# Two attentions of a fused block: units of four heads up to 256 keys, transposes two steps behind the scores, projection quarters in every short step

## The chip, the cores and the metric

The kernel runs on one core of one Trainium2 chip. The metric is device time in microseconds (us), the median of three runs of the kernel before: 1913.82 us (1909.85 to 1915.39). The profile shown is one further execution. Engines are named as the profile names them: PE is TensorE (PEld its weight loads), DVE is VectorE, ACT is ScalarE, POOL is GpSimd, SP is SyncE, which here only issues DMAs.

## The reference, cut to what matters

512 tokens of width 1024 pass four layers in turn. The change touches the attention of the last two. In both, twelve mixing heads of 64 columns (causal with a forget gate in the third layer, dilated in the fourth) and four memory heads over 256 memory tokens end in the same projection:

```python
sc = jnp.einsum('bhqd,bhkd->bhqk', qi, k) * scale       # per block of 128 queries
sc = sc + ci[..., :, None] - c[..., None, :]            # third layer: cumulated log forget gates
sc = jnp.where(kpos[None, :] <= qpos[:, None], sc, NEG)
p = jax.nn.softmax(sc, axis=-1)
out = jnp.einsum('bhqk,bhkd->bhqd', p, v)
...
heads = jnp.concatenate([mix, mem_out], axis=1)
h = h + merge_heads(heads) @ w_out[layer]
h = h + conv_ffn(rmsnorm(h, norm_ffn[layer]), ...)
```

The fourth layer's three dilated branches come to one causal softmax with a table of added logarithms, so both layers share one code path.

## The kernel before

`attn34` (from line 1246) is called twice, for the third and the fourth layer. It projects queries, keys, values and memory, then walks the attention proper (lines 1373 to 1478).

Work is cut into units (line 1454): a block of 128 queries, in the order 3, 2, 0, 1 (line 1453), and a pair of heads `j` (eight pairs; 6 and 7 are the memory heads). A unit of block `qb` has 128, 256, 384 or 512 keys, a memory pair always 256: 32 units in all. The loop of line 1456 makes one step a unit, 34 steps:

- `score` of unit i (line 1382): two matmuls, one for each head on half of the rows of the array, two more that add the forget gates in the third layer; the result lies in a tile `spp` of two PSUM banks, of which there are two. DVE adds the mask and takes the minimum of the negated scores (line 1404; memory heads line 1408), ACT takes the exponential and its sum (line 1409), DVE the reciprocal (line 1412) and the scaled probability (line 1414), in a tile `p2` a head, four of them.
- `value` of unit i - 2 (line 1428): matmuls of values and transposed probabilities into a bank `o` that four pairs share. After the fourth, `group` (line 1441) splits the bank into a high part on ACT (line 1445) and a low part on DVE (line 1446), for a projection in three matmuls.
- `turn_p` of unit i - 1 (line 1416): PE transposes the probabilities into one of two banks `tps`, and `evac` copies them to a tile `pt`, two times in three on ACT (line 361), else on DVE (line 359).
- `steps.tick()` (line 1476): work put off by so many ticks. After the second group of a block `finish` (line 868) is put off by three (line 1449); it makes the output projection in quarters of 24 matmuls of 256 columns, one a tick, into the one bank `misc`, adds two halves to the residual (line 891), then normalises the block (squares on ACT, line 241; sums, a power on POOL, products, lines 242 to 247). Four ticks later the normalised block is transposed in two halves of four, each half through `misc`, and split by ACT and DVE (lines 266 to 270). The last block uses the bank `o` for its second half and leaves its transposes to the next layer's start.

PE's order is written by hand: `Chain` (line 330) makes each score, value, transpose and projection matmul follow the one before it. The transposes of the normalised block and everything on DVE, ACT and POOL are not in the chain; a scheduler places them by program order and readiness. A tile waits until its buffer is free. The projection's weights are loaded and split (lines 204 and 206) while the first units run.

Of the kernel before, what the change touches and what calls it, by code (L numbers as in the profile page):

```python
# [97 lines left out]
def _build(tc, nc, ctx, t, out, dbg, upto):  # L98
    V, A, G, PE = nc.vector, nc.scalar, nc.gpsimd, nc.tensor
# [10 lines left out]
    nrm = pool(ctx, "nrm", 1)  # L110
# [14 lines left out]
    def pst(tag):  # L125
        return banks[tag].tile([128, 512], F32, tag=tag, name=tag)
# [274 lines left out]
    pp = phase(pst_, "prep", side="right")  # L401
# [45 lines left out]
    for half in range(2):  # L447
# [9 lines left out]
        for q in range(2):  # L457
# [8 lines left out]
            tp = pst("ft")  # L466
# [26 lines left out]
    pt = pp.tile([128, 3, 16], F32, name="pt")  # L493
# [287 lines left out]
    steps = Steps()  # L781
# [128 lines left out]
    steps = Steps()  # L910
    chain = Chain()
# [74 lines left out]
    units = [(qb, kv) for qb in range(NB - 1, -1, -1) for kv in range(2)]  # L986
    sts = {qb: {} for qb in range(NB)}
# [258 lines left out]
    def attn34(li, x3, w_in, w_out_ap, gain_next):  # L1246
# [132 lines left out]
        steps = Steps()  # L1379
        chain = Chain()  # L1380

        def score(qb, j, st_):
            qs = slice(qb * 128, qb * 128 + 128)
            nm, sm = st_["nm"], st_["sm"]
            m = 128 * (qb + 1) if j < 6 else 256
            rows = [slice(i * 64, i * 64 + 64) for i in range(2)]
            forget = li == 0 and j < 6
            pp = spp()
            for i, rw in enumerate(rows):
                if j < 6:  # L1390
                    chain.matmul(pp[:, i, :m], qT[rw, j, qs], kT[rw, j, :m], start=True, stop=not forget)
                else:
                    chain.matmul(pp[:, i, :m], qmT[rw, j - 6, qs], kmT[rw, j - 6], start=True, stop=True)
            if forget:
                for i in range(2):
                    chain.matmul(pp[:, i, :m], sel[rows[i], 2 * j + i:2 * j + i + 1].to_broadcast([64, 128]),
                                 c24[rows[i], :m], start=False, stop=True)
            h2 = slice(2 * j, 2 * j + 2)
            for i in range(2):
                hd = 2 * j + i  # L1400
                p2 = ae.tile([128, 512], F32, tag="p2", name="p2", bufs=4)
                src = pp[:, i]
                if j < 6:
                    V.tensor_tensor_reduce(out=p2[:, :m], in0=src[:, :m], in1=nlm[:, 512 - m:], scale=1.0,
                                           scalar=3e38, op0=OP.add, op1=OP.min, accum_out=nm[:, hd:hd + 1])
                    src = p2
                else:
                    V.tensor_reduce(nm[:, hd:hd + 1], src[:, :m], axis=AX.X, op=OP.min)
                A.activation(p2[:, :m], src[:, :m], AF.Exp, bias=nm[:, hd:hd + 1], scale=-1.0,  # L1409
                             accum_out=sm[:, hd:hd + 1])  # L1410
                st_[hd] = p2
            V.reciprocal(sm[:, h2], sm[:, h2])
            for hd in (2 * j, 2 * j + 1):
                V.tensor_scalar(st_[hd][:, :m], st_[hd][:, :m], sm[:, hd:hd + 1], None, op0=OP.mult)

        def turn_p(qb, j, st_):
            m = 128 * (qb + 1) if j < 6 else 256
            st_["pt", j] = []
            for i in range(2):
                p2 = st_[2 * j + i]  # L1420
                tp = tps()
                for kb in range(m // 128):
                    chain.transpose(tp[:, kb * 128:(kb + 1) * 128], p2[:, kb * 128:(kb + 1) * 128], ident)
                pt_ = ae.tile([128, 512], F32, tag="pt", name="pt_", bufs=2)
                evac(pt_[:, :m], tp[:, :m])
                st_["pt", j].append(pt_)

        def value(qb, j, st_):
            m = 128 * (qb + 1) if j < 6 else 256
            jj = j % 4  # L1430
            if jj == 0:
                st_["po", j // 4] = pst("o")
            pov = st_["po", j // 4].rearrange("p (j q) -> p j q", j=4)
            for kb in range(m // 128):
                for i in range(2):
                    hd = 2 * j + i
                    vv = vt[:, kb, hd * 64:(hd + 1) * 64] if j < 6 else vm[:, kb, (hd - 12) * 64:(hd - 11) * 64]
                    chain.matmul(pov[i * 64:(i + 1) * 64, jj], vv, st_["pt", j][i][:, kb * 128:(kb + 1) * 128],
                                 start=kb == 0, stop=kb == m // 128 - 1)

        def group(qb, hg, st_):
            po = st_["po", hg]
            ah = ap_.tile([128, 4, 128], F32R, tag="ah", name="ah", bufs=3)
            al = ap_.tile([128, 4, 128], F32R, tag="al", name="al", bufs=3)
            A.activation(f3(ah), po, AF.Copy)
            V.tensor_tensor(f3(al), po, f3(ah).bitcast(F32), op=OP.subtract)
            st_["a", hg] = (ah, al)
            if hg == 1:
                steps.later(3, lambda: finish(
                    steps, wo, lambda k: (st_["a", k // 4][0][:, k % 4], st_["a", k // 4][1][:, k % 4]), qb, gb, xn_,  # L1450
                    qb == order[-1], ap_ if order.index(qb) % 2 else nrm, chain))

        order = (3, 2, 0, 1)
        units = [(qb, j) for qb in order for j in range(8)]
        sts = {qb: {} for qb in range(NB)}
        for i in range(len(units) + 2):
            if i in (1, 2):
                q = int(i == 2)
                ps = pst("misc")
                fm(ps, w, q * 128, 128, xk(x3))  # L1460
                A.activation(qmT[:, q], ps, AF.Copy, scale=-0.125)
            if i < len(units):
                qb, j = units[i]
                if j == 0:
                    sts[qb]["nm"] = ae.tile([128, 16], F32, tag="nm", name="nm", bufs=2)
                    sts[qb]["sm"] = ae.tile([128, 16], F32, tag="sm", name="sm", bufs=2)
                score(qb, j, sts[qb])
# [174 lines left out]
```

## Time and profile before

| what | us |
|---|---|
| median of three runs (1909.85 to 1915.39) | 1913.82 |
| the profiled execution | 1911.97 |
| its span, first to last instruction | 1910.2 |
| attention of the third layer, first score matmul to first projection matmul of the last block | 732.65 to 867.40 |
| attention of the fourth layer, the same | 1381.30 to 1519.04 |

Times within the span are counted from its start. In rows of a stretch, the first number is its length, then the busy time of each engine with its number of instructions; a busy PE need not be PE at its peak, since matmuls are pipelined and their ends modelled. PEclk is the share of full clock that the throttle granted.

### The profile page before, as it was taken

How to read it: one execution, taken by the hardware profiler on the slowest of the kernel's cores; microseconds unless marked ns; L12 is line 12 of the kernel's file. 1: busy time of each engine (PE TensorE's matmuls, PEld its weight loads, DVE VectorE, ACT ScalarE, POOL GpSimd, SP SyncE). 2: the span in 40 equal slices, each digit the busy share in tenths (PEclk: the TensorE clock that was granted, in tenths of full speed). 3: DMA queues.
4: the chain of work that ended last, by engine and by line, in shares of the span. 5: the costliest groups of instructions: out<-in, count | busy, mean ns of one | idle time of the engine just before them, and what ended most of it. 6: DMA issues, size and time to landing. Idle time of an engine off the chain costs nothing.

```text
span 1910.2 us, 27945 instructions
## 1 busy us (share of the span) xinstructions
PE 1806.0 (95%) x11106; PEld 1512.9 (79%) x11108; DVE 1043.8 (55%) x2201; ACT 731.5 (38%) x1456; POOL 139.3 (7%) x151
## 2 busy tenths in 40 slices
PE   6799799999999999999999999999989999999998
PEld 5787578768789886778888888899957788888886
DVE  5985564279555534655655563265375565554522
ACT  4233353333443334543443342133264444333421
POOL 1452001213120000000000000000000000000000
PEclk9899989969999999999999999999998999999999
DMA  5303412301512442003333323342220043332321
GB/s 176 100 24 100 142 36 62 100 22 57 179 54 75 125 122 77 13 1 91 102 107 89 89 81 106 100 144 93 69 84 1 3 130 103 89 94 83 110 88 67
DMA packets 187899, 161.75 MB, mean 85 GB/s; under 512 B 14568, under 2 KB 170320, under 8 KB 187768
## 3 DMA queue, kind: packets, MB, share of 16 engines
q1 hardware_dynamic: 181168, 144.30, 24.6%
q0 software_dynamic: 2784, 9.00, 1.6%
q10 hardware_dynamic: 3816, 6.66, 1.1%
q8 instruction: 88, 1.44, 0.3%
q14 instruction: 43, 0.35, 0.1%
HBM read 157.88 MB, written 4.74 MB: 85 GB/s over the span
## 4 chain that ended last, share of the span: by engine, by line
PE 76%; DVE 10%; issue 5%; ACT 4%; DMA 3%; POOL 2%; ACTq 0%; POOLq 0%; DVEq 0%; SPq 0%
PE acc L212 19%; PE acc L210 19%; PE acc L211 19%; PE misc L339 6%; PE o L339 3%; PE tps L339 2%; PE spp L339 2%; DVE wl L206 2%; PE sps L1096 1%; ACT wh L204 1%; PE misc L210 1%; POOL rstd L234 1%; PE misc L211 1%; PE misc L212 1%; ACT p L1409 1%
## 5 line engine op out<-in xcount | busy, mean ns | idle before, releaser
L206 DVE TENSOR_TENSOR wl<-raw,wh 128x1024 fp32r<-128x1024 f32 (+3 forms) x250 | 300.6, 1211 | 402.6 <-ACT wh L204 401.9
L204 ACT ACTIVATE wh<-raw 128x1024 fp32r<-128x1024 f32 (+2 forms) x262 | 270.8, 1044 | 483.3 <-PE acc L211 211.6
L212 PE MATMUL acc<-xh,wl 128*128 128x512 f32 (+2 forms) x1064 | 400.4, 377 | 4.9 <-DVE wl L206 4.9
L210 PE MATMUL acc<-xh,wh 128*128 128x512 f32 (+2 forms) x1064 | 401.1, 379 | 1.2 <-ACT wh L204 0.7
L211 PE MATMUL acc<-xl,wh 128*128 128x512 f32 (+2 forms) x1064 | 400.5, 377 | 1.2 <-DVE xl L270 1.0
L212 PEld LDWEIGHTS acc<-xh,wl 128*128 128x128 f32 (+1 forms) x1064 | 200.5, 188 | 45.6 <-DVE wl L206 6.5
L210 PEld LDWEIGHTS acc<-xh,wh 128*128 128x128 f32 (+1 forms) x1064 | 199.8, 189 | 41.0 <-ACT wh L204 1.1
L211 PEld LDWEIGHTS acc<-xl,wh 128*128 128x128 f32 (+1 forms) x1064 | 200.5, 189 | 39.7 <-DVE xl L270 1.2
L210 PE MATMUL acc<-wh,xh 128*128 128x256 f32 (+1 forms) x704 | 206.5, 294 | 12.3 <-DVE u L359 10.2
L212 PE MATMUL acc<-wh,xl 128*128 128x256 f32 (+1 forms) x704 | 202.9, 288 | 0.6 <-DVE xl L270 0.6
L211 PE MATMUL acc<-wl,xh 128*128 128x256 f32 (+1 forms) x704 | 201.7, 287 | 0.9 <-DVE wl L206 0.9
L210 PEld LDWEIGHTS acc<-wh,xh 128*128 128x128 f32 x704 | 136.2, 193 | 17.5 <-DVE u L359 10.4
L212 PEld LDWEIGHTS acc<-wh,xl 128*128 128x128 f32 x704 | 136.2, 193 | 5.7 <-issue 4.4
L212 PE MATMUL acc<-wh,gl 128*128 128x512 f32 x352 | 139.2, 395 | 0.0
L210 PE MATMUL acc<-wh,gh 128*128 128x512 f32 x352 | 138.5, 394 | 0.0
L211 PE MATMUL acc<-wl,gh 128*128 128x512 f32 x352 | 138.5, 393 | 0.0
L211 PEld LDWEIGHTS acc<-wl,xh 128*128 128x128 f32 x704 | 136.3, 194 | 1.8 <-DVE wl L206 1.1
L245 POOL TENSOR_TENSOR rs<-ss,mhalf 128x1 f32<-128x1 f32 x32 | 17.6, 551 | 1463.8 <-DVE ss L243 1447.7
L339 PE MATMUL misc<-wh,ah 128*128 128x256 f32 x280 | 82.4, 294 | 0.0
L339 PE MATMUL misc<-wl,ah 128*128 128x256 f32 x280 | 79.4, 283 | 0.0
L339 PE MATMUL misc<-wh,al 128*128 128x256 f32 x280 | 79.1, 282 | 0.0
L211 PEld LDWEIGHTS acc<-wl,gh 128*128 128x128 f32 x352 | 66.2, 188 | 15.6
(1501 smaller groups left out, 3065.9 us busy)
## 6 DMA issues: line engine op xcount, KB each, us to landing
raw<-in_w_up_dram SPq DMA_DIRECT2D x176, 256.0 KB, 3.2
raw<-in_w_down_dram SPq DMA_DIRECT2D x44, 512.0 KB, 3.6
raw<-in_od_w_in_dram SPq DMA_DIRECT2D x24, 512.0 KB, 3.6
raw<-in_w_in_dil_dram SPq DMA_DIRECT2D x20, 512.0 KB, 3.9
raw<-in_ev_w_in_dram SPq DMA_DIRECT2D x18, 512.0 KB, 4.3
raw<-in_w_out_dram SPq DMA_DIRECT2D x16, 512.0 KB, 3.8
raw<-in_w_in_fox_dram SPq DMA_DIRECT2D x14, 512.0 KB, 4.3
raw<-in_ev_w_out_dram SPq DMA_DIRECT2D x8, 512.0 KB, 4.2
```

Of the source, the lines that this page charges most:

```text
L204: A.activation(hi[:, k0:k1], raw, AF.Copy)
L206: eng.tensor_tensor(lo[:, k0:k1], raw, hi[:, k0:k1].bitcast(F32), op=OP.subtract)
L210: pe.matmul(ps, lh, rh, start=first, stop=False)
L211: pe.matmul(ps, lh, rl, start=False, stop=False)
L212: pe.matmul(ps, ll, rh, start=False, stop=last)
L234: G.tensor_tensor(r2[:, :n], r[:, :n], mhalf[:, :n], op=OP.pow)
L245: G.tensor_tensor(r, ss[:, 3:4], mhalf[:, :1], op=OP.pow)
L339: self.last = op(*a, **k).ins
L1096: PE.matmul(ps[:, :n], qiT[rw, hd // 2, qs], kiT[rw, :n], start=True, stop=True)
L1409: A.activation(p2[:, :m], src[:, :m], AF.Exp, bias=nm[:, hd:hd + 1], scale=-1.0, accum_out=sm[:, hd:hd + 1])
```

## The change

A unit becomes a block and a tuple of head pairs: one pair as before for the mixing heads of blocks 2 and 3, two pairs (four heads) for the memory heads of every block and for all heads of blocks 0 and 1. Two pairs lie side by side in the columns of the same `spp`, `p2`, `tps` and `pt` tiles. A step now makes the score of unit i, the value of unit i - 3 and the transposes of unit i - 2; `p2` has six buffers. `finish` is put off by one tick, which is the tick of the same step, and the normalised block always lies in the tile of the pool `nrm`, which has one buffer, where it alternated with a second tile. The quarters of the projection come one a tick, as before.

```diff
+        def width(qb, js):
+            return 128 * (qb + 1) if js[0] < 6 else 256
+
+        def score(qb, js, st_):
...
+            m = width(qb, js)
...
+            forget = li == 0 and js[0] < 6
+            cols = [slice(a * m, a * m + m) for a in range(len(js))]
             pp = spp()
...
+            for j, cl_ in zip(js, cols):
+                for i, rw in enumerate(rows):
+                    if j < 6:
+                        chain.matmul(pp[:, i, cl_], qT[rw, j, qs], kT[rw, j, :m], start=True, stop=not forget)
+                    else:
+                        chain.matmul(pp[:, i, cl_], qmT[rw, j - 6, qs], kmT[rw, j - 6], start=True, stop=True)
+                if forget:
+                    for i in range(2):
+                        chain.matmul(pp[:, i, cl_], sel[rows[i], 2 * j + i:2 * j + i + 1].to_broadcast([64, 128]),
+                                     c24[rows[i], :m], start=False, stop=True)
+            ps_ = [ae.tile([128, 512], F32, tag="p2", name="p2", bufs=6) for _ in range(2)]
+            for j, cl_ in zip(js, cols):
                 for i in range(2):
...
-                p2 = ae.tile([128, 512], F32, tag="p2", name="p2", bufs=4)
...
+                    hd = 2 * j + i
+                    p2, src = ps_[i][:, cl_], pp[:, i, cl_]
+                    if j < 6:
+                        V.tensor_tensor_reduce(out=p2, in0=src, in1=nlm[:, 512 - m:], scale=1.0,
+                                               scalar=3e38, op0=OP.add, op1=OP.min, accum_out=nm[:, hd:hd + 1])
+                        src = p2
+                    else:
+                        V.tensor_reduce(nm[:, hd:hd + 1], src, axis=AX.X, op=OP.min)
+                    A.activation(p2, src, AF.Exp, bias=nm[:, hd:hd + 1], scale=-1.0, accum_out=sm[:, hd:hd + 1])
+            h2 = slice(2 * js[0], 2 * js[-1] + 2)
             V.reciprocal(sm[:, h2], sm[:, h2])
...
+        def turn_p(qb, js, st_):
+            n = width(qb, js) * len(js)
...
+            for p2 in st_["p", js]:
                 tp = tps()
-                for kb in range(m // 128):
+                for kb in range(n // 128):
...
-                evac(pt_[:, :m], tp[:, :m])
+                evac(pt_[:, :n], tp[:, :n])
...
+        def value(qb, js, st_):
+            nk = width(qb, js) // 128
+            if js[0] % 4 == 0:
+                st_["po", js[0] // 4] = pst("o")
...
+            for a, j in enumerate(js):
+                for kb in range(nk):
+                    for i in range(2):
...
+                        ks = slice((a * nk + kb) * 128, (a * nk + kb + 1) * 128)
+                        chain.matmul(pov[i * 64:(i + 1) * 64, j % 4], vv, st_["pt", js][i][:, ks],
+                                     start=kb == 0, stop=kb == nk - 1)
...
             if hg == 1:
-                steps.later(3, lambda: finish(
+                steps.later(1, lambda: finish(
                     steps, wo, lambda k: (st_["a", k // 4][0][:, k % 4], st_["a", k // 4][1][:, k % 4]), qb, gb, xn_,
-                    qb == order[-1], ap_ if order.index(qb) % 2 else nrm, chain))
+                    qb == order[-1], nrm, chain))
 
         order = (3, 2, 0, 1)
-        units = [(qb, j) for qb in order for j in range(8)]
+        units = [(qb, js) for qb in order
+                 for js in ([(0, 1), (2, 3), (4, 5)] if qb < 2 else [(j,) for j in range(6)]) + [(6, 7)]]
         sts = {qb: {} for qb in range(NB)}
-        for i in range(len(units) + 2):
+        for i in range(len(units) + 3):
...
-            if i > 1:
-                qb, j = units[i - 2]
-                value(qb, j, sts[qb])
-                if j % 4 == 3:
-                    group(qb, j // 4, sts[qb])
-            if 0 < i <= len(units):
-                qb, j = units[i - 1]
-                turn_p(qb, j, sts[qb])
+            if i > 2:
+                qb, js = units[i - 3]
+                value(qb, js, sts[qb])
+                if js[-1] % 4 == 3:
+                    group(qb, js[-1] // 4, sts[qb])
+            if 1 < i <= len(units) + 1:
+                qb, js = units[i - 2]
+                turn_p(qb, js, sts[qb])
             steps.tick()
```

## Rows read from the trace of the kernel before

**Rows 1.** The page, part 1: busy us (share of span) and instructions by engine

```profile
PE 1806.0 (95%) x11106; PEld 1512.9 (79%) x11108; DVE 1043.8 (55%) x2201; ACT 731.5 (38%) x1456; POOL 139.3 (7%) x151
```

**Rows 2.** Stretches of the third layer's attention: length, busy us, clock, DMA

```profile
749.12:770.11 20.99, 17.16 (x120) 10.99 (x119) 16.68 (x39) 13.76 (x29) 0.00 (x0) 0.84 0.50 151
802.83:813.04 10.21, 8.27 (x76) 5.61 (x75) 8.34 (x32) 6.70 (x24) 0.55 (x1) 1.00 0.00 0
813.04:829.85 16.81, 16.59 (x143) 14.70 (x142) 7.80 (x36) 6.35 (x28) 0.00 (x0) 1.00 0.00 1
829.85:840.25 10.40, 8.93 (x75) 6.02 (x74) 9.17 (x32) 7.12 (x24) 0.55 (x1) 1.00 0.01 2
859.72:867.40 7.68, 5.44 (x45) 3.57 (x44) 5.42 (x12) 3.72 (x11) 0.55 (x1) 1.00 0.01 2
```

**Rows 3.** Stretches of the fourth layer's attention, each from a first score matmul

```profile
1394.58:1415.67 21.09, 16.77 (x142) 10.59 (x141) 18.68 (x40) 16.50 (x32) 0.00 (x0) 1.00 0.47 150
1448.41:1460.92 12.51, 10.50 (x69) 6.70 (x68) 8.61 (x32) 6.65 (x24) 0.55 (x1) 0.75 0.00 0
...
1478.97:1491.84 12.87, 10.85 (x70) 6.37 (x69) 9.55 (x34) 7.60 (x25) 0.55 (x1) 0.87 0.00 1
1510.35:1519.03 8.68, 6.55 (x45) 4.45 (x44) 5.75 (x13) 3.45 (x10) 0.55 (x1) 0.83 0.01 2
```

**Rows 4.** PE's timeline from 1448.41: start, duration, line, operation, idle before

```profile
1449.05 0.32 PE L339 MATMUL o<-pt__13462,vt 128*64 128x128 f32 x1
...
1449.85 0.66 PE L339 MATMUL tps<-ident,p 128*128 128x128 f32 x4
1450.44 0.49 PE L339 MATMUL spp<-kT,qT 64*128 64x128 f32 x4
1450.86 0.43 PE L339 MATMUL o<-pt__13526,vm 128*64 128x128 f32 x2
...
1451.79 0.63 PE L266 MATMUL misc<-ident,xn 128*128 128x128 f32 x4
1453.83 0.66 PE L266 MATMUL misc<-ident,xn 128*128 128x128 f32 x4 [1.41 <-DVE xl L270]
```

**Rows 5.** PE's timeline of a tight step, from 1478.97

```profile
1479.60 0.32 PE L339 MATMUL o<-pt__13788,vt 128*64 128x128 f32 x1
...
1479.97 0.66 PE L339 MATMUL tps<-ident,p 128*128 128x128 f32 x4
1480.56 0.70 PE L339 MATMUL spp<-kT,qT 64*128 64x256 f32 x4
```

**Rows 6.** Waits of PE, third layer's attention: total us, times, longest

```profile
PE tps L339 <- DVE p L1414: 2.5, 7, 0.7
PE misc L266 <- DVE xl L270: 1.4, 1, 1.4
PE o L339 <- ACT pt__7377 L361: 1.1, 1, 1.1
```

**Rows 7.** Waits of PE, fourth layer's attention

```profile
PE tps L339 <- DVE p L1414: 4.5, 8, 0.9
PE misc L266 <- DVE xl L270: 2.8, 2, 1.4
```

**Rows 8.** Timeline: last value matmul of a group, and the group's split on DVE

```profile
793.86 0.27 PE L339 MATMUL o<-pt__7705,vt 128*64 128x128 f32 x1
...
796.76 0.68 DVE L1446 TENSOR_TENSOR al<-o,ah 128x512 fp32r<-128x512 f32 x1
...
1422.80 0.27 PE L339 MATMUL o<-pt__13200,vm 128*64 128x128 f32 x1
...
1424.24 0.68 DVE L1446 TENSOR_TENSOR al<-o,ah 128x512 fp32r<-128x512 f32 x1
```

**Rows 9.** Copies of transposes on DVE, 512 and 256 columns: busy us, mean ns

```profile
L359 DVE COPY pt__7495<-tps 128x512 f32<-128x512 f32 x1 | 0.7, 690 | 1.0 <-PE tps L339 1.0
L359 DVE COPY pt__8218<-tps 128x256 f32<-128x256 f32 x1 | 0.4, 425 | 0.3 <-PE tps L339 0.3
```

More of the change, by code (lines that the diff above doesn't have):

```diff
@@ L1380, in attn34 @@
         chain = Chain()
-        def score(qb, j, st_):
+        def width(qb, js):
+            return 128 * (qb + 1) if js[0] < 6 else 256
+        def score(qb, js, st_):
             qs = slice(qb * 128, qb * 128 + 128)
             nm, sm = st_["nm"], st_["sm"]
-            m = 128 * (qb + 1) if j < 6 else 256
+            m = width(qb, js)
             rows = [slice(i * 64, i * 64 + 64) for i in range(2)]
-            forget = li == 0 and j < 6
+            forget = li == 0 and js[0] < 6
+            cols = [slice(a * m, a * m + m) for a in range(len(js))]
@@ L1388, in score @@
             pp = spp()
[L1389 to L1394, printed above, removed]
-                for i in range(2):
-                    chain.matmul(pp[:, i, :m], sel[rows[i], 2 * j + i:2 * j + i + 1].to_broadcast([64, 128]),
-                                 c24[rows[i], :m], start=False, stop=True)
@@ L1398, in score @@
-            h2 = slice(2 * j, 2 * j + 2)
-            for i in range(2):
-                hd = 2 * j + i
-                p2 = ae.tile([128, 512], F32, tag="p2", name="p2", bufs=4)
[L1402 to L1411, printed above, removed]
@@ L1412, in score @@
-            V.reciprocal(sm[:, h2], sm[:, h2])
[L1413 to L1420, printed above, removed]
+            for j, cl_ in zip(js, cols):
[8 more added lines that the diff above has]
+                                     c24[rows[i], :m], start=False, stop=True)
@@ L1421, in turn_p @@
+            h2 = slice(2 * js[0], 2 * js[-1] + 2)
+            V.reciprocal(sm[:, h2], sm[:, h2])
+            for j, cl_ in zip(js, cols):
+                for i in range(2):
+                    hd = 2 * j + i
+                    V.tensor_scalar(ps_[i][:, cl_], ps_[i][:, cl_], sm[:, hd:hd + 1], None, op0=OP.mult)
+            st_["p", js] = ps_
+        def turn_p(qb, js, st_):
+            n = width(qb, js) * len(js)
+            st_["pt", js] = []
+            for p2 in st_["p", js]:
                 tp = tps()
-                for kb in range(m // 128):
+                for kb in range(n // 128):
@@ L1423, in turn_p @@
                     chain.transpose(tp[:, kb * 128:(kb + 1) * 128], p2[:, kb * 128:(kb + 1) * 128], ident)
                 pt_ = ae.tile([128, 512], F32, tag="pt", name="pt_", bufs=2)
-                evac(pt_[:, :m], tp[:, :m])
[L1426 to L1439, printed above, removed]
+                evac(pt_[:, :n], tp[:, :n])
@@ new lines, in turn_p @@
+                st_["pt", js].append(pt_)
+        def value(qb, js, st_):
+            nk = width(qb, js) // 128
+            if js[0] % 4 == 0:
+                st_["po", js[0] // 4] = pst("o")
+            pov = st_["po", js[0] // 4].rearrange("p (j q) -> p j q", j=4)
+            for a, j in enumerate(js):
+                for kb in range(nk):
+                    for i in range(2):
+                        hd = 2 * j + i
+                        vv = vt[:, kb, hd * 64:(hd + 1) * 64] if j < 6 else vm[:, kb, (hd - 12) * 64:(hd - 11) * 64]
+                        ks = slice((a * nk + kb) * 128, (a * nk + kb + 1) * 128)
+                        chain.matmul(pov[i * 64:(i + 1) * 64, j % 4], vv, st_["pt", js][i][:, ks],
+                                     start=kb == 0, stop=kb == nk - 1)
@@ L1462, in attn34 @@
             if i < len(units):
-                qb, j = units[i]
-                if j == 0:
+                qb, js = units[i]
+                if js[0] == 0:
                     sts[qb]["nm"] = ae.tile([128, 16], F32, tag="nm", name="nm", bufs=2)
                     sts[qb]["sm"] = ae.tile([128, 16], F32, tag="sm", name="sm", bufs=2)
-                score(qb, j, sts[qb])
-            if i > 1:
-                qb, j = units[i - 2]
-                value(qb, j, sts[qb])
-                if j % 4 == 3:
-                    group(qb, j // 4, sts[qb])
-            if 0 < i <= len(units):
-                qb, j = units[i - 1]
-                turn_p(qb, j, sts[qb])
+                score(qb, js, sts[qb])
+            if i > 2:
[6 more added lines that the diff above has]
+                turn_p(qb, js, sts[qb])
             steps.tick()
```

## The prediction

> **What bounds the kernel now.** The first part of the page gives the share of each engine: TensorE (PE) is busy for 95% of the span [rows 1]. That says little about the two attentions, because the end of a matmul is modelled and a short one counts for longer than it holds the array. So I cut each attention into stretches at the first score matmul of a step (a pass of the unit loop) and asked for the busy time of each engine in them. The reader is to see three kinds of stretch. Where every step carries a quarter of the output projection, PE idles 0.22 us in 16.81 us for four steps [rows 2]: nothing to win. Where the first query block (512 keys) runs beside the splitting of the projection's weights, VectorE (DVE) is busy 16.68 of 20.99 us in the first attention and 18.68 of 21.09 us in the second [rows 2, 3]: DVE sets most of that pace. Between two projections, and behind the last unit, PE idles in both: 1.94 of 10.21 us, 2.01 of 12.51 us and so on [rows 2, 3]. There the granted TensorE clock also drops: it is 0.75, 0.87 and 0.83 over three such stretches of the second attention, so part of each ran at 1.2 instead of 2.4 GHz after PE had idled [rows 3].
>
> The timeline tells what such a step should take. A tight one, of two heads without projection, starts its scores at 1478.97, where a stretch begins [rows 3], its values at 1479.60, its transposes at 1479.97 and the next scores at 1480.56: 0.63 + 0.37 + 0.59 = 1.59 us [rows 5]. Another, from 1448.41, goes 0.64 + 0.80 + 0.59 us with six value pairs instead of two [rows 3, 4], so a value pair costs (0.80 - 0.37) / 4 = 0.108 us and the group a fixed 0.15. Scores for 128 keys take 0.42 us [rows 4] against 0.63 for 256, so 0.21 per 128 keys and 0.21 fixed. Four transposes at about the price of a value pair are 0.43, so of their 0.59 some 0.16 is fixed (an estimate). **A two-head step thus pays about 0.52 us for changing from scores to values to transposes and back**, whatever its width.
>
> With these prices I rebuild the stretches. The four steps from 1448.41 are 2.03 + 1.59 + 1.37 + 1.16 = 6.15 us, the eight transposes of the normalised block 8 x 0.11 = 0.88; measured 12.51, so 5.5 us are waits [rows 3, 4]. The same sum gives 7.0 + 0.88 of 12.87 (waits 5.0) for the other stretch [rows 3], and in the first attention, whose scores have a third matmul pair (0.06 to 0.12 us more), 6.3 + 0.88 of 10.21 (waits 3.0) and 7.35 + 0.88 of 10.40 (2.2) [rows 2]. Together 15.7 us in sixteen steps. Behind the last unit (scores, three value groups, two transpose groups, the eight transposes: 4.43 us) the stretches last 7.68 and 8.68 us: 3.25 + 4.25 = 7.5 us of waits [rows 2, 3]. **So 23.2 us of waits stand in six short stretches.** Who is late: the transposes wait for the scaled probabilities, 2.5 us in seven places and 4.5 us in eight [rows 6, 7], and the second half of the normalised block waits 1.41 us for the copy of the first out of the one bank "misc" [rows 4, 7]. The rest is values that wait for the copied transposes.
>
> **The change part by part.** No matmul, exponential or byte of DMA is added; PE's order is written by hand (the chain), and nothing passes another instruction on SP's queue, and POOL has only the power of each norm, as before.
>
> *Four-head units.* Units fall from 32 to 7 + 7 + 4 + 4 = 22 for each attention: ten score, value and transpose groups less in each, 20 in both. At 0.52 us that is 10.4 us at most, and 0 at least, if a merged unit pays the fixed part again between its two head pairs, which no row shows. The tight steps all show the fixed part at a change of kind, so I take a value near the upper end: **-8 us**. The copies of the transposes become half as many and twice as wide (0.69 us for 512 columns, 0.42 for 256 [rows 9]); the reciprocals halve. Both lie on DVE and ScalarE (ACT) beside a PE that is the bound in steps with a quarter: 0. If that cover goes, a copy is 0.27 us later.
>
> On that the Trainium skill speaks against the change: "Perfetto Trace Analysis", section "Optimizing Scalar/DVE Operations", says that when those engines are not saturated but cause bubbles elsewhere, breaking instructions up helps, and grouping pays when they are. The trace has DVE busy for 8.34 of 10.21 us there [rows 2], nearer to the second condition. By the first, six merged steps without a quarter would lose 6 x 0.27 = 1.6 us, and the sum below would be -18.4 instead of -20.0.
>
> *Quarters in every short step.* With two fewer ticks before `finish` and four steps for a block, the quarters fill steps 9 to 12 and then 16 to 27 of a loop of 25 and its drain; before they filled 11 to 14, 19 to 22, 27 to 30 and 35 to 38. The sixteen waiting steps become six without a quarter (13 to 15 in each attention), and the last values and transposes go between quarters. What stays of the 23.2 us: the six steps at 0.8 us (15.7 / 16 = 1.0 now, less 0.2 since a whole step more lies before the transposes): 4.8 us. And the eight transposes of query block 2 now fall between the last quarter of block 0 and the first of block 1, all through "misc": the residual add (0.69 by the width of the other 512-column DVE rows), then twice 2.04 us from half to half [rows 4], 4.8 us in all, of which 0.88 is work and 1.0 covered by the values of the last unit (0.15 + 8 x 0.108): 2.9 us, twice 5.8. So 23.2 - 10.6 = **-12.6 us**, with bounds of -18.4 (no squeeze) and -7.5 (the tails alone).
>
> *Transposes two steps behind, six probability tiles.* The waits for scaled probabilities add up to 7.0 us [rows 6, 7], most of them in the stretches counted already. Outside, DVE at 80 to 89% stays what it is [rows 2, 3], and the values still come one step behind the transposes, so the wait passes on to the copies: **-1 us**, bounds 0 and -4. The two more tiles hold the unit that is now in flight; scores still wait for the two score banks, as before.
>
> *The first quarter in the step of its group.* Its first 12 matmuls read the older half of the heads; the other 12 need the split of the group just finished. From the last value matmul to the end of the split 2.12 us pass in one place (1422.80 to 1424.92) and 3.58 in another (793.86 to 797.44) [rows 8]. Transposes (0.59) and half a quarter (a step with quarter is 16.81 / 4 = 4.2 us [rows 2], a step like it without 1.2, so 1.5 for the half) cover 2.1 us. Bounds 0 and 1.5 us for each of eight blocks; the later one had norm work on ACT ahead of it, the earlier not. Of the eight groups those of blocks 0 and 1 come one step behind a norm: 0.4 each for these four, 0 for the others, **+1.6 us**. Queued behind that wait on PE are the next scores, by the chain.
>
> *One normalised tile for all blocks.* Block 0's squares must wait for block 2's transposes; by the count above they end 4.8 us after block 0's last quarter, and the result is needed only behind quarters of 3 us each: 0. If that cover went, the squares, two small sums, the power on POOL and the two products would stand in a row, and the start of the next layer's work would wait.
>
> Sum: -8 - 12.6 - 1 + 1.6 = **-20.0 us** against the profiled execution's 1911.97 us (span 1910.2 and 1.8 around it; 1.85 under the median 1913.82 of the three runs): **1892 us**. A measurement of this kernel can tell about 0.3% (5.7 us) from no change.
>
> **The rivals.**
>
> *The wait moves on (1905.6).* The probabilities are ready sooner, but the copies behind them are not, and every wait of the six stretches reappears one engine later, in the steps with a quarter. Only the removed steps count: -8 + 1.6 = -6.4. For it: in the 512-key stretch late copies stand in front of values, the longest by 1.1 us [rows 6], and DVE is 80 to 89% busy. Against it: steps with a quarter show no such waits today [rows 2]. Chance 0.20. With one squeeze more in each attention it is no change (1912), chance 0.13, which also holds the case that the order on DVE and ACT, which is not written by hand, undoes the longer lag.
>
> *"misc" becomes the bound (1920).* From step 16 on that bank carries quarters without a pause, and all three blocks' transposes must squeeze through it, each pair costing 0.69 + 2 x 2.04 = 4.8 us of which 0.9 is work. If none is covered, that is 6 x 3.9 = 23.4 us, where such pairs cost 1.4 + 2.8 = 4.2 now by waits of this kind [rows 6, 7]. The scores stand behind the blocked quarter in the chain, so of the gain only the removed steps and a part of the tails (-5 of 7.5) are left: -8 + 1.6 - 5 + 23.4 - 4.2 = +7.8. It decides once a pair costs more than 3 us and the lag wins nothing. Against it: those transposes are outside the chain and stand a step or two ahead of their place in the program today [rows 4]. Chance 0.08. The Trainium skill ("Perfetto Trace Analysis", section "Matmuls") asks independent groups to rotate through banks, so that the copy of one overlaps the matmuls of the next; the 1.41 us idle [rows 4] agree with what happens otherwise.
>
> *More than counted (under 1881).* No wait left and the clock at 2.4 GHz throughout: -10.4 - 18.4 - 4 = -33, 1879. Chance 0.04.
>
> **How the numbers follow.** The forecast (1881 to 1900) has 0.55, the moved wait 0.20, no change 0.13, slower 0.08, more 0.04. Faster by over 0.3%: 0.55 + 0.20 + 0.04 = 0.79; within it 0.13; slower 0.08. The range runs from 1881 to 1909, past the first rival.
>
> **What would show it.** Right: the stretches with all units of 128 and 256 keys have PE idle under 1 us in ten, the clock row stays near 1.00 from the second block on, and "tps waits for p L1414" falls from 7.0 to under 2 us. The squeeze: a wait of "misc" quarters for the copies of the normalised block, near the end of each attention. Wrong: the same idle time with the copies of transposes as releasers, or first quarters that wait for the split by over 1 us.

## The result and the profile after

The changed kernel takes 1900.9 us (median of six runs, 1897.92 to 1905.28) against 1910.8 beside it: ratio 0.9942, 95% interval 0.993 to 0.9954. Its profiled execution took 1900.18 us, the one of before 1911.97. First the page's part 1, to be held against [rows 1]: PE is busy for 14.7 us less in all.

```profile
PE 1791.3 (94%) x11108; PEld 1513.8 (80%) x11108; DVE 1036.1 (55%) x2167; ACT 728.5 (38%) x1430; POOL 138.8 (7%) x151
```

The two profiled executions, cut at the start of an attention's first score matmul, of its last projection matmul, and of the first Silu of the feed-forward behind it (us; worked out from the timelines; attention 4 is cut at 1380.76 before, its first score matmul, a half microsecond ahead of the 1381.30 of the table above):

| | to attention 3 | attention 3 | to Silu | to attention 4 | attention 4 | to Silu | rest |
|---|---|---|---|---|---|---|---|
| before | 732.65 | 146.03 | 29.06 | 473.02 | 149.73 | 29.66 | 349.99 |
| after | 735.41 | 149.70 | 25.96 | 473.49 | 137.87 | 25.95 | 349.98 |

Attention 4 gained 11.9 us, **attention 3 lost 3.7**, and 3.1 + 3.7 us came from the start of the feed-forwards, which the forecast had at nothing. (The first column and the fourth are code that the change does not touch. Over all kept traces of this document they take 732.65 to 738.76 and 472.21 to 476.73 us, so differences of a few us there say nothing.) A part of the difference between the two attentions is PE's clock: it stood at its lower level for 6.8 and 17.1 us of them before, for 13.7 and 3.4 us after.

Stretches of the changed kernel, with the columns of [rows 2, 3]. The first covers five steps near the start of attention 3; those from 813.03 and 1448.37 begin at a first score matmul; the last begins behind the transposes of block 2's normalised block:

```profile
747.42:770.62 23.20, 18.15 (x138) 12.16 (x136) 17.52 (x38) 16.42 (x31) 0.00 (x0) 0.93 0.44 136
...
813.03:826.92 13.89, 9.08 (x62) 7.92 (x62) 5.59 (x23) 4.65 (x17) 0.00 (x0) 0.77 0.00 0
...
1448.37:1459.82 11.45, 9.73 (x90) 6.96 (x89) 9.44 (x38) 8.16 (x30) 0.55 (x1) 1.00 0.01 2
1507.28:1512.60 5.32, 4.09 (x34) 3.98 (x34) 3.40 (x7) 3.72 (x7) 0.55 (x1) 1.00 0.04 12
```

At the start DVE is busy for 17.52 of 23.20 us, five steps; in [rows 2] for 16.68 of 20.99, four steps. One step of attention 3, from 813.03, takes 13.89 us at a mean clock of 0.77, where the step behind it, with a quarter as well, takes 5.2. The main waits of PE in attention 3, then in attention 4 (total us, times, longest), against [rows 6, 7]:

```profile
PE misc L266 <- DVE xl L270: 4.4, 2, 3.4
PE o L339 <- DVE pt__7355 L359: 4.3, 1, 4.3
PE misc L339 <- DVE xl L270: 2.6, 2, 1.4
PE o L339 <- DVE al L1454: 1.8, 2, 1.4
...
PE misc L339 <- DVE al L1454: 1.1, 2, 0.9
```

```profile
PE o L339 <- DVE al L1454: 2.6, 2, 1.4
PE o L339 <- ACT pt__12918 L361: 2.6, 1, 2.6
PE misc L266 <- DVE xl L270: 2.3, 2, 1.2
...
PE misc L339 <- DVE xl L270: 1.2, 1, 1.2
PE misc L339 <- DVE al L1454: 0.9, 2, 0.7
```

The wait for scaled probabilities, 7.0 us before, is gone from both attentions. Others have grown. Values wait 11.6 us for copied transposes, 9.4 before (the sums of all such waits in both attentions), and 4.4 us for the split that empties their bank "o" (`al`), 0.8 before. The bank "misc" costs 4.4 + 2.6 + 2.3 + 1.2 = 10.5 us of waits around the transposes of normalised blocks. The long step of attention 3 on PE's timeline (start, duration, line, operation, idle before):

```profile
815.77 0.27 PE L266 MATMUL misc<-ident,xn 128*128 128x128 f32 x1
819.44 0.66 PE L266 MATMUL misc<-ident,xn 128*128 128x128 f32 x4 [3.40 <-DVE xl L270]
821.50 0.58 PE L339 MATMUL misc<-wh,ah 128*128 128x256 f32 x1 [1.41 <-DVE xl L270]
821.88 0.41 PE L339 MATMUL misc<-wl,ah 128*128 128x256 f32 x1
822.10 0.41 PE L339 MATMUL misc<-wh,al 128*128 128x256 f32 x1
```

The last transpose of block 3's first half starts at 815.77; the second half can start only at 819.44 and the first quarter of block 2 at 821.50. Its matmuls then come every 0.21 us where they come every 0.12 elsewhere: the trace has the clock at half from 820.4 to 827.2. The quarter takes 5.42 us, to the next scores, where others take 3.0. What the first half's copy (the last line) stood behind, on DVE:

```profile
816.98 0.87 DVE L1421 TENSOR_SCALAR p<-p,sm 128x128 f32<-128x128 f32 x4
817.77 0.68 DVE L1454 TENSOR_TENSOR al<-o,ah 128x512 fp32r<-128x512 f32 x1
818.37 0.41 DVE L359 COPY pt__7977<-tps 128x256 f32<-128x256 f32 x1
818.70 0.68 DVE L270 TENSOR_TENSOR xl<-misc,xh 128x512 fp32r<-128x512 f32 x1
```

And the start of the feed-forward behind attention 4, DVE's timeline before, then after:

```profile
1530.81 0.69 DVE L891 TENSOR_TENSOR h<-o,h 128x512 f32<-128x512 f32 x1 [4.02 <-PE o L339]
1531.42 1.22 DVE L206 TENSOR_TENSOR wl<-raw,wh 128x1024 fp32r<-128x1024 f32 x1
```

```profile
1511.46 2.35 DVE L206 TENSOR_TENSOR wl<-raw,wh 128x1024 fp32r<-128x1024 f32 x2
1514.72 0.69 DVE L891 TENSOR_TENSOR h<-misc,h 128x512 f32<-128x512 f32 x1 [0.91 <-PE misc L339]
```

Before, the first up-projection slab (a tile of weights) was split (`wl`) behind the last block's last residual add, and PE waited 2.0 us in three places for such splits. After, both pieces of it are split ahead of the first half's add, and PE has no such wait.

### The profile page after: what moved, and what is told of

Its sections match the earlier page's. It is cut to its first block, busy times and chain, and to the rows that moved or that the text cites. A ratio compares the mean times of both kernels' runs of the same rounds, so it can differ in the third digit from the quotient of the medians.

```text
span 1898.4 us, 27786 instructions
## 1 busy us (share of the span) xinstructions
PE 1791.3 (94%) x11108; PEld 1513.8 (80%) x11108; DVE 1036.1 (55%) x2167; ACT 728.5 (38%) x1430; POOL 138.8 (7%) x151
## 4 chain that ended last, share of the span: by engine, by line
PE 78%; DVE 8%; issue 5%; ACT 4%; DMA 3%; POOL 1%; ACTq 0%; POOLq 0%; DVEq 0%; SPq 0%
PE acc L212 20%; PE acc L210 20%; PE acc L211 20%; PE misc L339 6%; PE o L339 3%; PE tps L339 2%; DVE wl L206 1%; PE spp L339 1%; PE sps L1096 1%; DMA raw<-in_w_in_dil_dram 1%; ACT wh L204 1%; ACT p L1415 1%; PE misc L210 1%; PE misc L211 1%; PE misc L212 1%
## 5 line engine op out<-in xcount | busy, mean ns | idle before, releaser
L210 PEld LDWEIGHTS acc<-wh,xh 128*128 128x128 f32 x704 | 135.9, 193 | 18.4 <-DVE u L359 10.4
L210 PE MATMUL acc<-wh,gh 128*128 128x512 f32 x352 | 138.5, 394 | 0.0
L211 PE MATMUL acc<-wl,gh 128*128 128x512 f32 x352 | 138.5, 393 | 0.0
```

The source lines that it names most:

```text
L210: pe.matmul(ps, lh, rh, start=first, stop=False)
L211: pe.matmul(ps, lh, rl, start=False, stop=False)
```

## The experiments

Ratios are to the kernel before, timed on the same chip in the same rounds. Its median beside store_only to x_by_tps is 1915.6, beside lag_one_x to store_x 1915.2, beside empty_tile to lag_one_x_pool 1911.3, beside x_a_step_earlier 1914.8. Stage lengths of every profiled execution:

| run | ratio (95%) | attention 3 | to Silu | attention 4 | to Silu |
|---|---|---|---|---|---|
| the change | 0.9942 (0.993 to 0.9954) | 149.70 | 25.96 | 137.87 | 25.95 |
| store_only | 0.9943 (0.9926 to 0.9961) | 143.98 | 25.77 | 152.99 | 25.77 |
| pairs | 0.997 (0.9958 to 0.9982) | 149.14 | 25.77 | 146.47 | 25.77 |
| lag_one | 0.99 (0.9886 to 0.9915) | 143.10 | 25.42 | 142.01 | 25.73 |
| x_by_tps | 0.9888 (0.9874 to 0.9903) | 140.38 | 26.00 | 138.03 | 26.00 |
| lag_one_x | 0.9881 (0.9861 to 0.9902) | 141.02 | 25.77 | 138.46 | 26.00 |
| lag_one_p4 | 0.997 (0.9954 to 0.9985) | 141.49 | 31.26 | 138.76 | 32.03 |
| x_lo_on_pool | 0.9883 (0.9863 to 0.9904) | 140.25 | 25.76 | 135.20 | 25.77 |
| store_x | 1.004 (1.0025 to 1.0055) | 150.75 | 25.78 | 154.07 | 26.00 |
| empty_tile | 0.9957 (0.9943 to 0.997) | 144.06 | 25.76 | 146.78 | 25.77 |
| lag_only | 0.9972 (0.9958 to 0.9986) | 145.77 | 25.95 | 147.58 | 25.70 |
| lag_one_x_pool | 0.9881 (0.9867 to 0.9894) | 139.67 | 25.76 | 139.58 | 25.77 |
| x_a_step_earlier | 0.9947 (0.9933 to 0.9961) | 146.98 | 26.02 | 142.18 | 25.77 |

The attentions of the kernel before, of store_only and of empty_tile have the same instructions on PE in the same order; they took 144.0 to 146.0 and 146.8 to 153.0 us. So one attention of one execution is good to some 3 us, and the starts of the feed-forward (25.4 to 26.0 wherever they are early) to a few tenths.

**store_only**: the storage alone, on the kernel before.

```diff
-                p2 = ae.tile([128, 512], F32, tag="p2", name="p2", bufs=4)
+                p2 = ae.tile([128, 512], F32, tag="p2", name="p2", bufs=6)
...
-                    qb == order[-1], ap_ if order.index(qb) % 2 else nrm, chain))
+                    qb == order[-1], nrm, chain))
```

> The kernel before with only the storage of the change: six probability tiles and one normalised tile; units, lag and quarters as before, PE's order in the two attentions unchanged. Theory A (the feed-forward starts gained 3.1 and 3.7 us in the changed kernel because the six probability tiles push the projection's weights out of the memory of the first up-projection slab, so that its splits no longer stand behind the last block's residual add): about 1904 to 1905 against 1911 (ratio 0.9965), all of it between the last projection matmul and the first Silu (29.1 and 29.7 become about 26). Rival B (those 6.8 us come from the earlier norm of block 0, that is from the units and quarters): no difference (ratio 1.000), the stretches stay at 29.

Both starts fell to 25.77: theory A. The median fell further than these 7.2 us (1902.6 from 1915.6); the ratio's interval, 7.5 to 14.2 us, begins just above them, and no trace here shows where the rest comes from. **The storage alone is worth about as much as the whole change.**

**empty_tile**: the kernel before with one normalised tile, four probability tiles, and beside them memory that nothing uses.

```diff
         ae = phase(stx, "ae")
+        ae.tile([128, 1024], F32, tag="pad", name="pad", bufs=1)
```

> The kernel before with one normalised tile and an empty tile of 4096 bytes a partition, which nothing reads or writes, beside its four probability tiles: the memory of six tiles without the tiles. Units, lag, quarters and PE's order in the attentions as before. If it is the place of the projection's weights in memory that starts the feed-forward earlier: 25.8 us in both starts instead of 29.1 and 29.7, 1902 to 1905 in all, as with six tiles (0.9943). If two more tiles to write into gave the gain: 1910 to 1914 and starts of 29.

The starts are 25.76 and 25.77. The kernel needs the place, not the tiles (nor is it the one normalised tile: lag_one_p4 below has it too, without the place, and starts late). DVE's timeline of this run has the split of the slab ahead of the adds, as after the change:

```profile
1517.24 2.36 DVE L206 TENSOR_TENSOR wl<-raw,wh 128x1024 fp32r<-128x1024 f32 x2 [1.68 <-ACT wh L204]
1520.05 0.69 DVE L891 TENSOR_TENSOR h<-misc,h 128x512 f32<-128x512 f32 x1 [0.46 <-PE misc L339]
```

The code agrees: the pool `ae` with six probability tiles, two copies and its small sums is 16,640 bytes a partition, exactly the two tiles of the slab in the pool `wx`, which takes that place next; with four it is 4,096 less, and the slab reaches into the pool `wo`, which holds weights of the projection that is still running.

**lag_one**: transposes one step behind the scores, as before the change.

```diff
-        for i in range(len(units) + 3):
+        for i in range(len(units) + 2):
...
-            if i > 2:
-                qb, js = units[i - 3]
+            if i > 1:
+                qb, js = units[i - 2]
...
-            if 1 < i <= len(units) + 1:
-                qb, js = units[i - 2]
+            if 0 < i <= len(units):
+                qb, js = units[i - 1]
```

> The changed kernel with the transposes one step behind the scores as before (a loop one step shorter); four-head units, six tiles, first quarter in the step of its group stay. By the forecast's term the lag is worth 1 us: 1901 to 1903 (changed kernel: 1901). If the lag is what lets the merged units work, the waits of transposes for scaled probabilities come back (7 us before, nearly none now) and it is 1905 to 1908. If the copies are late anyway, the longer lag only costs its extra step at the end and this is 1898 to 1900.

1896.2 us, below all three: the interval of the ratio, 0.9886 to 0.9915, lies under that of the change, so the longer lag made the change slower. In attention 3 its long step takes 6.79 us, not 13.89, since the scheduler placed block 3's transposes a step sooner. (Attention 4 of this profile takes 142.0 us, 4 more than in the change.)

**lag_one_p4**: lag_one with `bufs=4` for `p2`.

> The kernel with transposes one step behind, with four probability tiles instead of six (one step of lag needs no more). It takes away only the storage. Theory A (six tiles keep the first up-projection slab clear of the projection's weights): both feed-forward starts go back from 25.4 and 25.7 to about 29, the attentions stay within 3 us of 143 and 142, in all 6 to 8 us over the 1896 of six tiles: 1902 to 1904. Rival B (the starts come from the units and quarters): 25.5 to 26 stay, 1896.

The starts went to 31.26 and 32.03, the time to 1906.8: theory A, at nearly twice the price. In the start behind attention 4 PE waits 0.9 us for splits on DVE and 3.4 for those on ACT; the longest of these waits, 2.8 us, ends with a split before which ACT had idled 4.88 us for the weights' DMA. Units and early quarters without the storage are worth 0.3%.

**pairs**: two heads a unit again.

```diff
-                 for js in ([(0, 1), (2, 3), (4, 5)] if qb < 2 else [(j,) for j in range(6)]) + [(6, 7)]]
+                 for js in [(j,) for j in range(8)]]
```

> The changed kernel with units of two heads everywhere; lag of two steps, six tiles, one normalised tile and first quarter in the step of its group stay. It takes away the merged units and with them the quarters in every short step. Theory A: what is left is the storage (-6.5) and the lag with the earlier quarters (-1 to -4 in the two attentions): 1901 to 1904. By the terms of the forecast (units -8, quarters in every short step -12.6, nothing for storage) only -1 would be left: 1910. If it is as fast as the changed kernel (1900 to 1901), the merged units gave nothing net.

0.997, 1909.4: some 6 us under before, where the storage alone gives 11 (0.9943; 8 by empty_tile). So without merged units, lag and earlier quarters together cost some 3 to 5 us, which neither figure of the expectation had; that 1910 came near is luck, since the storage's gain was missing in it and this cost as well. The run also shows what a merged unit saves. 256 keys with a quarter, two heads here (PE's timeline: scores, first value matmul, transposes, quarter), then four heads in the changed kernel:

```profile
1498.12 0.70 PE L339 MATMUL spp<-kT,qT 64*128 64x256 f32 x4
1498.75 0.32 PE L339 MATMUL o<-pt__13982,vt 128*64 128x128 f32 x1
...
1499.34 0.66 PE L339 MATMUL tps<-ident,p 128*128 128x128 f32 x4
1499.75 0.36 PE L339 MATMUL misc<-wh,ah 128*128 128x256 f32 x1
```

```profile
1487.87 1.14 PE L339 MATMUL spp<-kmT,qmT 64*128 64x256 f32 x8
1488.93 0.32 PE L339 MATMUL o<-pt__13782,vt 128*64 128x128 f32 x1
...
1489.96 1.09 PE L339 MATMUL tps<-ident,p 128*128 128x128 f32 x8
1490.81 0.36 PE L339 MATMUL misc<-wh,ah 128*128 128x256 f32 x1
```

Two of the first take 2 x 1.63 = 3.26 us before the quarter, one of the second 2.94: 0.32 saved, not 0.52. In front of a quarter the transposes show next to no fixed part (0.41 for four, 0.85 for eight).

**lag_only**: store_only with the loop of the change, one step longer (`units[i - 3]`, `units[i - 2]`).

> The kernel before with the storage and with the transposes two steps behind the scores; two-head units, first quarter two steps behind its group as before. The forecast put the lag at -1: 1901 to 1904, with the storage at 0.9943. If the lag moves the waits from the transposes to the scores and adds a step (two-head units with lag and early quarters took 0.997, so about 5 us more than the storage alone): 1907 to 1910, and the scores' waits grow from some 24 to over 30 us in both attentions.

0.9972, 1906.0, between the two ranges expected: by the ratios 3 us slower than empty_tile beside it, whose interval overlaps, and 6 slower than store_only. The waits for scores did not grow either (22.7 us, 24.4 in store_only). The waits for probabilities are gone (7.6 us in empty_tile), and the values' waits for copies go from 9.2 to 14.5 us, with one of 4.2 us in attention 3:

```profile
PE o L339 <- DVE pt__7355 L359: 4.2, 1, 4.2
```

From the first score to the first quarter it takes 51.8 and 53.1 us, against 49.2 in both attentions of empty_tile; but that quarter comes a step later by the code, so this is not all loss. These sums do not add up to the 3 to 6 us, and the rest stays open.

**x_by_tps**: the changed kernel, with a normalised block's transposes in the two banks of the probability transposes.

```diff
-                norm_block(h[:, tb], gb, x, tb, ("misc", "misc"), pl, lambda f: steps.later(4, f))
+                norm_block(h[:, tb], gb, x, tb, ("tps", "tps"), pl, lambda f: steps.later(4, f))
```

> The changed kernel with the eight transposes of a normalised block through the two banks of the probability transposes instead of the one bank of the quarters; the scheduler then places them inside quarters. Theory C (attention 3 loses because the transposes of block 3 squeeze through the bank of the quarters at step 16: 3.67 + 1.68 us of waits, then a quarter at half clock 2.4 us longer; block 2's squeeze 1.3 to 1.5 each): about -8 to -10, 1891 to 1893, the step of the first quarter of block 2 in attention 3 falls from 13.9 us to under 7. Rival D (VectorE and ScalarE are late with the copies, wherever these lie): the probability transposes wait for their banks instead, 1899 to 1903.

1893.4, ratio 0.9888: theory C. In attention 3, block 3's transposes now lie inside the quarter, with its matmuls between them:

```profile
821.87 0.60 PE L266 MATMUL tps<-ident,xn 128*128 128x128 f32 x4
...
823.34 0.60 PE L266 MATMUL tps<-ident,xn 128*128 128x128 f32 x4
```

That step takes 7.06 us, and the gap between the last projection matmul of block 0 and the first of block 1 falls from 5.36 to 1.23 us in both attentions. (The edit is shown by its effect; it holds for the last two attentions only.)

**store_x**: the same two banks, in store_only.

> The kernel before with the storage of the change (six probability tiles, one normalised tile) and with the transposes of a normalised block through the two banks of the probability transposes; two-head units, lag and quarters as before. In the storage kernel the gaps between the projections of two blocks took 11.9, 12.8, 7.9 us (attention 3) and 13.1, 18.6, 8.0 us (attention 4). If the waits of the kernel before between two projections were mostly the one bank, the gaps shrink by 2 to 3 us each and it is 1890 to 1895, so that the units and quarters of the change are worth little beside it. If these waits are the scaled probabilities and the copies, as the forecast had it, it gains 2 to 4 us over the storage alone: 1899 to 1901.

Both were wrong: 1.004, 18 us slower than store_only. The probability transposes wait longer for the scaled probabilities (attention 3, then attention 4; 1.9 and 5.0 us in store_only):

```profile
PE tps L339 <- DVE p L1414: 5.6, 6, 2.3
```

```profile
PE tps L339 <- DVE p L1414: 8.5, 8, 2.5
```

The four longest of them (1.93, 2.30, 2.22 and 2.50 us) come in steps where, in store_only, transposes of a normalised block stood ahead of the probability transposes and took up the time. Here they come behind. The end of attention 4 on PE's timeline, store_only, then store_x:

```profile
1513.75 0.63 PE L266 MATMUL misc<-ident,xn 128*128 128x128 f32 x4 [0.32 <-DVE xn L247]
1515.79 0.66 PE L266 MATMUL misc<-ident,xn 128*128 128x128 f32 x4 [1.41 <-DVE xl L270]
1516.28 0.67 PE L339 MATMUL tps<-ident,p 128*128 128x128 f32 x4
```

```profile
1528.48 0.92 PE L339 MATMUL tps<-ident,p 128*128 128x128 f32 x4 [2.50 <-DVE p L1414]
...
1530.04 0.69 PE L266 MATMUL tps<-ident,xn 128*128 128x128 f32 x2
```

The two attentions of the profile are 7.9 us longer than those of store_only, about what these four waits come to; the rest of the 18 us is not accounted for.

So the other banks helped in the change, where the transposes came to lie inside quarters, and cost time in the kernel with pairs, where they left a wait uncovered.

**x_a_step_earlier**: the changed kernel, `steps.later(3, f)` for these transposes, in "misc".

> The changed kernel with the transposes of a normalised block due three steps behind its norm instead of four, still through the bank of the quarters. PE's order keeps block 3's transposes where they were (in front of block 2's first quarter) and moves block 2's between the second and the third quarter of block 0, out of the gap in front of block 1. If the one bank is the cost wherever no matmuls cover the copies: that gap falls from 5.4 to about 1.2 us in both attentions, the quarters of block 0 get longer by 3 to 4 us, nothing is won (1898 to 1902), and attention 3 keeps its long step of 13 to 14 us in front of block 2. If only the place behind block 0's last quarter was bad: 1893 to 1896.

0.9947, 1903.2. Block 2's squeeze moved and was not won, as the bank theory has it: the gap is 1.23 us in both attentions, the quarters of block 0 take 25.1 and 25.2 us instead of 19.5. The other half was wrong: the long step of attention 3 fell to 7.25 us through the same bank. There the last transpose of block 3's first half starts at 816.00, before the scores of that step, and its copies run beside them.

**lag_one_x**: lag_one with the two banks. **x_lo_on_pool** and **lag_one_x_pool**: x_by_tps and lag_one_x with `ring["lo"] = G` around `wout_slabs` (line 205 then makes half of the low parts on POOL).

> The changed kernel with both: transposes one step behind the scores, and the transposes of a normalised block through the two banks of the probability transposes. If the lag costs time by itself (an extra step at the end, more work in flight) and the one bank costs time by itself, the two add up: the attentions take 136 to 138 us each, 1888 to 1891 in all. If the gain of the lag of one (1896 against 1901) was only that its step order spared attention 3 the squeeze in the bank of the quarters, nothing is left to add: 1893 to 1895, as with the two banks alone.

> The changed kernel with the transposes of a normalised block through the two banks of the probability transposes, and half of the low parts of the projection's weights (4 of 8 in each attention) made on POOL instead of VectorE. It asks what binds the first stretch, from the first score to the first quarter (47.2 and 46.6 us with the two banks alone, 46.3 and 44.5 in the changed kernel). If VectorE binds it: 4 x 1.2 us less on VectorE in each attention, 42 to 44 us there, 1885 to 1890 in all. If ScalarE or the arrival of the weights binds it, or POOL slows VectorE down: 46 or more, 1893 or slower.

> The changed kernel with transposes one step behind, those of a normalised block through the two banks of the probability transposes, and half of the low parts of the projection's weights on POOL. The first two gave 0.9881, the last two 0.9883, against 0.9888 for the banks alone. If the first stretch is bound by VectorE with a lag of one too: 1885 to 1888 (0.985 to 0.987). If it is bound by the arrival of the weights or by ScalarE: 1890 (0.988).

All three ratios lie within the interval of x_by_tps; the medians are 1890.0, 1890.1 and 1889.1. Once the bank is free, no clear gain of the lag of one is left: 1890.0 lies in the range given for two costs that add up, but the attentions took 141.0 and 138.5 us, not 136 to 138. First score to first quarter, x_by_tps, then x_lo_on_pool (length, PE, PEld, DVE, ACT, POOL, clock):

```profile
738.76:785.99 47.23, 40.40 (x279) 27.47 (x278) 32.67 (x82) 28.24 (x63) 0.00 (x0) 0.93 0.30 90
1378.18:1424.78 46.60, 39.61 (x264) 26.70 (x264) 32.83 (x82) 29.68 (x65) 0.00 (x0) 0.93 0.30 91
```

```profile
735.19:782.27 47.08, 41.43 (x279) 28.24 (x278) 29.58 (x78) 28.52 (x64) 9.61 (x4) 0.93 0.29 90
1377.21:1421.66 44.45, 39.48 (x265) 26.44 (x264) 28.38 (x78) 30.11 (x66) 10.01 (x4) 0.96 0.31 95
```

DVE is relieved of 3.1 and 4.5 us; attention 3 starts 0.2 us faster, attention 4 2.2 (the changed kernel, without the relief, has 46.3 and 44.5 us). So these runs do not show that busy DVE sets that pace by itself. In the changed kernel ACT's splits there wait for the weights' DMA (0.44 and 1.21 us at 755.55 and 759.01), with exponentials and copies queued behind them. That was not tested further.

## Why the prediction was right, and where it was not

The sign and the range held; the sum did not. It had -20.0 us in the attentions and nothing elsewhere. The profiled executions show -8.2 in the attentions and -6.8 at the two feed-forward starts, less 3.2 lost in stretches that the change does not touch. The 1900.9 us lie just past the forecast's own 1881 to 1900, and without the starts, which the forecast did not have, the profiled execution would stand at 1907.0, near the first rival's 1905.6: that the range held is in good part luck. Held against the storage alone, units, lag and quarters together are worth between nothing (0.9942 against store_only's 0.9943) and 3 us (against empty_tile's 0.9957).

- *Four-head units, -8*: right in size as far as the steps show. 20 groups at 0.32 (measured in front of a quarter) to 0.52 us (the prediction's estimate) are 6.4 to 10.4, nearer the lower end, since most merged units end in a quarter. No run has the merged units alone: pairs, which takes the quarters out of the short steps as well, has attentions 8.0 us longer than the change where the forecast had 20.6.
- *Quarters in every short step*, "23.2 - 10.6 = -12.6": **this step failed, in the 10.6 that it left.** (Its 23.2 us are what six stretches take beyond the prices of tight steps; by [rows 2, 3] PE is idle for 11.8 of them, and the rest holds the lower clock as well.) It had eight transposes of block 2 squeeze through "misc" (2.9 us each) and gave block 3 no squeeze. Block 3 had one in attention 3: 3.40 + 1.41 us of waits and 2.4 us of quarter at half clock, 7.2 in all. Block 2's are the gaps of 5.4 us less values (1.0) and transposes (0.9), 3.5 each, 1.1 more in both than counted. Behind the one in attention 3 the clock fell too: that quarter takes 4.44 us, the same one in attention 4, behind the same waits, 2.93. So the term was 8 to 10 us too large. x_by_tps, which takes the three squeezes away (14.2 us), brings the attentions from 287.6 to 278.4, that is 9.2 us less, in an execution whose two starts took 3.0 longer; they then stand 17.4 us under the profiled run of before.
- *Transposes two steps behind, -1*: "the wait passes on to the copies" is what happened, but the price has the other sign. Alone it cost 3 to 6 us (lag_only against the storage), in the change itself 0.4% (lag_one, 0.99 against 0.9942); beside free banks nothing clear (lag_one_x).
- *Six probability tiles*: the forecast gave them only the unit in flight. Their place in memory gives 7 us of stage time, which empty_tile shows without the tiles. This term was missing.
- *First quarter in the step of its group, +1.6*: the waits for the split are 1.1 + 0.9 = 2.0 us in four places, of blocks 3 and 0, not 0 and 1. Right in size.
- *One normalised tile, 0*: right. In attention 3 block 0's squares start at 870.43, behind block 2's last copy on ACT and 3.5 us after their input is there (866.95); its transposes at 881.45 and 884.38 show no idle time before them. (In attention 4 the second half waits 1.21 us, for the bank "misc" and not for the tile.)
- The rule of the Trainium skill on breaking up instructions ("Perfetto Trace Analysis", section "Optimizing Scalar/DVE Operations"), as the prediction applied it, would have taken 1.6 us off the gain. Units as pairs were slower (0.997 against 0.9942), so in this kernel the grouped units paid; no run separates the wider copies from the rest of a unit.

The rival "misc becomes the bound" described the mechanism that did the harm, with 3.9 us for each block. It came for three of the six blocks and not for all; by x_by_tps (0.9888 against 0.9942) it took about half of the gain, not all of it.

## What to carry to other kernels

A tile count changes what lies beside it: before crediting a schedule with a gain, run the storage of the change alone, and an empty tile in its place. A bank that two kinds of work share cost nothing here only while other work of PE covered its copies. Moving transposes to other banks also moves them in PE's order: it won 0.5% in the changed kernel, where they came to lie inside quarters, and lost 1% in the kernel with pairs, where a wait that they had filled lay open. A longer lag did not make a late engine earlier; it moved the wait to the next tile.

## What had not been expected of the hardware

A wait of some 5 us on PE cost more than itself: between 820.4 and 827.2 the clock stood at its lower level (1.2 of 2.4 GHz) after PE had idled 3.40 us and while it idled another 1.41, and the quarter behind it took 5.42 us instead of 3.0. Yet the same idle times can go either way: PE idled 1.05 and 1.23 us in front of block 1's first quarter in both attentions, and the clock fell in attention 3 alone (871.6 to 875.0). And kernels with one and the same order of instructions on PE spread over 6 us in one attention, with the half-clock stretches at other places each time (in attention 4 of the kernel before from 1454.7, 1485.4 and 1516.1; in store_only from 1408.6, 1480.3 and 1517.8). The longer these are, the longer the attention: attention 4 has 6.8 us of them in empty_tile, 17.1 in the kernel before and 20.5 in store_only, and takes 146.8, 149.7 and 153.0 us. Single executions can't settle terms of a few us.
